# Last superblock of a hybrid decoder step: feed-forward tokens divided 512 + 320 instead of 384 + 448, final norm per piece

## The chip, the cores and the metric

The kernel runs on one core of one Trainium2 chip. The metric is device time in microseconds (us) of one execution, the median over several executions; lower is better. The profile names the engines PE (matrix multiply), PEld (its weight loads, which overlap the multiplies), DVE (vector), ACT (scalar), POOL (GpSimd) and SP (which issues the DMAs).

## The reference

One layer of a decoder trunk is computed for 2048 prompt tokens and 64 sample tokens, 1024 features each, all in fp32. The part that the change touches is the end of it:

```python
x = x + o @ w_co                      # end of the cross-attention
h = _rmsnorm(x, g_ffn)
x = x + jnp.square(jax.nn.relu(h @ w_up)) @ w_down     # hidden size 4096
...
y = _rmsnorm(x, g_final)
```

What comes before (a projection, windowed attention, a pooling mixer, cross-attention to 256 memory tokens) is not changed.

## The kernel before

Tokens stand along the free axis (columns), features on the 128 partitions, so x is 8 chunks of [128, tokens]. The tokens are worked through in three superblocks, each of two blocks (`SBLOCKS`): 384 + 384 tokens, then 256 + 256 with the 64 sample tokens, then 384 + 384. The residual x of a superblock lives in two SBUF tiles, `x_105` (block 0) and `x_106` (block 1). In the last superblock (s = 2) the 64 sample tokens, saved by superblock 1, are appended to block 1 in front of the feed-forward part, so that block 1 has `np` = 384 columns up to the cross stage and `nf` = 448 columns from there on.

Every fp32 product is made of three fp32r matmuls: weights and activations are each split into a rounded part (hi) and a remainder (lo), and hi*hi, hi*lo and lo*hi are summed in PSUM. In `dense` these are lines L317, L318, L319, in `mm3` lines L113, L114, L115. Each has its own 128x128 weight load. One weight tile pair (th, tl) of 128x1024 thus makes 24 matmuls for each block of tokens: 8 chunks of the contraction by 3 in `dense`; 2 output chunks of 4 contraction chunks by 3 in the down projection. I call these 24 matmuls a chunk.

The feed-forward part has groups g = 0 to 7. `up(g)` computes four hidden chunks for each feed-forward block `fb`; `down(g)` multiplies them by four weight tiles and adds them to x. The order is up(0), up(1), down(0), up(2), ..., up(7), down(6), down(7). In up(0), `head=2` does two chunks of one block, then two of the other; elsewhere the blocks alternate chunk by chunk. In down(7), the last, all four weight tiles are used for one block first, and then for the other, so that the first one's final norm runs beside the matmuls of the second. Before the change, superblock 2 has two feed-forward blocks that are the token blocks: 384 columns (block 0) and 448 (block 1); down(7) does block 1 first (`ends = (1, 0)`).

Each up chunk is evacuated by `up_evac`: DVE multiplies the relu of the PSUM tile by r3, the reciprocal norm of the tokens (L1192), ACT squares it (L1193) and rounds it (L1195), DVE makes the remainder (L1196). Down chunks are added to x by DVE (L1227). There are four PSUM tiles `mm` for the chunks. DVE and ACT also split each new weight tile (L135, L134).

`Act(n, nk)` lays out activations in SBUF tiles: pieces of 384 columns, four to a tile, for n up to 384, else pieces of 512 columns, three to a tile; `fb.more` lends the last feed-forward block of superblock 2 the tile `vt` and tiles of the weight pool `w` as additional room.

`Norm` sums squares of the 8 chunks. Off PE, ACT squares (L204, L207), DVE adds (L208), and one fp32 matmul by a matrix of ones (L216) sums over partitions. With `on_pe`, each square (L197) goes to PE at once (L200). `fin` then takes Ln and Exp on ACT (L219, L220) and a correction of three steps on DVE (L221 to L223). `final` applies it to the eight chunks of x on DVE (L1245) and issues four DMAs to y from SP (L1247).

Work that would stall an engine is put off: `later` holds pairs of a count and a function, and each `flush` counts down. `after_co(b)`, which finishes the norm r3 of block b, and `final` are put off in that way. The Tile framework then schedules the instructions on each engine by their dependencies; the order on an engine is fixed at build time.

Of the kernel before, what the change touches and what calls it, by code (L numbers as in the profile page):

```python
# [12 lines left out]
ALU = mybir.AluOpType  # L13
# [38 lines left out]
def kernel(ctx: ExitStack, tc: tile.TileContext, io, nW=12, nF=6, nT=8):  # L52
# [476 lines left out]
    def superblock(s, blks, nxt):  # L529
# [612 lines left out]
        def add_evac2(c, b, ps):  # L1142
            bl = blks[b]
            nc.vector.tensor_tensor(bl.x(c, 0, bl.np), ps[:, 0:bl.np], bl.x(c, 0, bl.np), ALU.add)
            fb, o = bl.fb, bl.fo
            gain(bl.xf(c), fb.h3.hi(c, o, o + bl.nf), fb.h3.lo(c, o, o + bl.nf), vec[:, V_GFFN + c:V_GFFN + c + 1])
            bl.norm.sq(c)

        def after_co(b):
# [3 lines left out]
            bl.norm.fin()  # L1153
            bl.r3 = bl.norm.r

        fbs = []
        for bl in blks:
            bl.norm = Norm(bl.nf, bl.xf)
            if not has or bl.b == 0:
                fb = FB()  # L1160
                fb.parts, fb.n, fb.more = [], 0, [(), (), ()]
                fbs.append(fb)
            bl.fb, bl.fo = fb, fb.n
            fb.parts.append(bl)
            fb.n += bl.nf
# [17 lines left out]
        def up_evac(g):  # L1183
            def f(c, b, ps):
                fb = fbs[b]
                if (g, b) not in hid:
                    hid[(g, b)] = Act(fb.n, 4, fb.more[1 + g % 2])
                H = hid[(g, b)]
                for bl in fb.parts:
                    o, n = bl.fo, bl.nf  # L1190
                    r, q = TS.get(), TS.get()
                    nc.vector.scalar_tensor_tensor(r[:, 0:n], ps[:, o:o + n], 0.0, bl.r3[:, 0:n], ALU.max, ALU.mult)  # L1192
# [12 lines left out]
        def down(g):  # L1205
            fin = g == 7
            nb = len(fbs)
            ends = (1, 0) if last else tuple(range(nb))
            seq = [(mp, b) for b in ends for mp in range(4)] if fin else [(mp, b) for mp in range(4) for b in range(nb)]
            loaded, left = {}, {}  # L1210
            if fin:
                for bl in blks:
                    bl.norm = Norm(bl.nf, bl.xf, on_pe=last and bl.b == 0)
            for mp, b in seq:
                if mp not in loaded:
                    loaded[mp] = S.next(("dn", s, g, mp))
# [5 lines left out]
                for m2 in range(2):  # L1222
                    m = 2 * mp + m2
                    ps = MM.get()
                    mm3(ps[:, 0:n], range(4), lambda k: w8(th)[:, 4 * m2 + k, :], lambda k: w8(tl)[:, 4 * m2 + k, :], H.hi, H.lo)
                    for bl in fb.parts:
                        nc.vector.tensor_tensor(bl.xf(m), ps[:, bl.fo:bl.fo + bl.nf], bl.xf(m), ALU.add)  # L1227
                        if fin:
                            bl.norm.sq(m)
# [11 lines left out]
        def final(bl):  # L1241
            bl.norm.fin()
            n, yo = bl.nf, 8 * bl.t0
            for k in range(8):
                nc.vector.scalar_tensor_tensor(bl.xf(k), bl.xf(k), vec[:, V_GFINAL + k:V_GFINAL + k + 1], bl.norm.r[:, 0:n], ALU.mult, ALU.mult)  # L1245
# [165 lines left out]
```

## Time and profile before

| what | value |
|---|---|
| median of 3 runs | 2584.61 us (2584.56 to 2587.79) |
| the profiled execution | 2587.05 us |
| its span, first to last instruction | 2585.3 us |
| PE busy | 2544.8 us, 98% of the span |
| DVE busy, ACT busy | 1376.7 us (53%), 994.1 us (38%) |
| mean granted PE clock | 0.994 of full speed |

The page's figures hold for the whole span; the feed-forward part of superblock 2 is the last 600 us or so of it (from 1981 us on). In the timeline a row gives start, duration, engine, line, operation, what it writes and reads, its shape. A matmul's duration is longer than the distance to the next one, since matmuls overlap in the array; the time that a matmul costs is the distance between starts.

### The profile page before, as it was taken

To read this page: it belongs to the slowest core of one execution; us is meant where nothing else is said; L and a number is where in the kernel's file an instruction comes from. 1 tells how busy PE (TensorE), PEld (TensorE's weight loads), DVE (VectorE), ACT (ScalarE), POOL (GpSimd) and SP (SyncE) were. 2 spreads that over 40 slices of the span, in tenths; PEclk is the share of its full clock that TensorE was granted. 3 is DMA by queue.
4 is the path that set the end of the run, shared out by engine and by line. 5 is a ranking of instruction groups with operands and counts; after the bars stand their busy time and mean duration, and the time that the engine had idled before them with its cause. 6 is when DMAs were issued, how large, how long until landed. Compare 5 with 4: busy or idle time off the path is not lost.

```text
span 2585.3 us, 35891 instructions
## 1 busy us (share of the span) xinstructions
PE 2544.8 (98%) x14239; PEld 2359.9 (91%) x14239; DVE 1376.7 (53%) x2643; ACT 994.1 (38%) x1931; POOL 169.4 (7%) x282
## 2 busy tenths in 40 slices
PE   8899999999999999999999999999999999999998
PEld 8798989999999999896888888899989999999997
DVE  8568535444434468763654546887445333333334
ACT  6666333322222234753442324475344322222221
POOL 0015010000000000411000000023010000000000
PEclk9999999999999999999999999999999999999999
DMA  7833212211112125156722222404111111111101
GB/s 283 257 125 105 87 36 82 66 66 63 61 66 66 50 65 159 50 175 212 274 97 98 98 98 74 157 24 145 41 66 62 61 58 58 57 58 58 58 25 53
DMA packets 96011, 245.06 MB, mean 95 GB/s; under 512 B 18852, under 2 KB 35684, under 8 KB 94820
## 3 DMA queue, kind: packets, MB, share of 16 engines
q1 hardware_dynamic: 95844, 242.78, 28.1%
q8 instruction: 112, 1.84, 0.3%
q14 instruction: 55, 0.45, 0.1%
HBM read 219.79 MB, written 22.95 MB: 94 GB/s over the span
## 4 chain that ended last, share of the span: by engine, by line
PE 56%; DVE 1%; ACT 1%; POOL 1%; DMA 1%; issue 0%; DVEq 0%; POOLq 0%; ACTq 0%
PE mm L318 10%; PE mm L319 10%; PE mm L317 10%; PE mm L113 7%; PE mm L114 7%; PE mm L115 7%; PE aux L724 1%; PE aux L755 1%; PE aux L1052 0%; DVE x L1245 0%; PE aux L968 0%; PE aux L113 0%; PE aux L115 0%; PE aux L114 0%; DVE w L135 0%
## 5 line engine op out<-in xcount | busy, mean ns | idle before, releaser
L317 PE MATMUL mm<-act,w 128*128 128x384 f32 (+4 forms) x2528 | 858.7, 340 | 2.0 <-ACT act L679 1.6
L319 PE MATMUL mm<-act,w 128*128 128x384 f32 (+4 forms) x2528 | 853.0, 337 | 1.9 <-DVE w L135 1.9
L318 PE MATMUL mm<-act,w 128*128 128x384 f32 (+4 forms) x2400 | 806.5, 336 | 0.2 <-DVE act L680 0.2
L134 ACT CAST w<-f 128x1024 fp32r<-128x1024 f32 x330 | 346.6, 1051 | 876.6 <-PE mm L114 281.2
L135 DVE TENSOR_TENSOR w<-f,w 128x1024 fp32r<-128x1024 f32 x330 | 402.8, 1225 | 221.2 <-PE mm L318 88.8
L113 PE MATMUL mm<-act,w 128*128 128x384 f32 (+3 forms) x1472 | 507.7, 345 | 3.9 <-ACT t L204 2.2
L115 PE MATMUL mm<-act,w 128*128 128x384 f32 (+3 forms) x1472 | 507.1, 345 | 1.9 <-DVE w L135 1.9
L317 PEld LDWEIGHTS mm<-act,w 128*128 128x128 f32 x2528 | 477.5, 189 | 21.4 <-ACT act L679 1.9
L319 PEld LDWEIGHTS mm<-act,w 128*128 128x128 f32 x2528 | 477.3, 189 | 17.3 <-DVE w L135 2.7
L318 PEld LDWEIGHTS mm<-act,w 128*128 128x128 f32 x2400 | 453.5, 189 | 17.5 <-issue 2.2
L114 PE MATMUL mm<-act,w 128*128 128x384 f32 (+3 forms) x1344 | 458.3, 341 | 0.0
L1227 DVE TENSOR_TENSOR x<-mm,x 128x384 f32<-128x384 f32 (+2 forms) x384 | 195.2, 522 | 294.9 <-PE mm L115 294.8
L113 PEld LDWEIGHTS mm<-act,w 128*128 128x128 f32 x1472 | 277.8, 189 | 20.7 <-ACT t L204 2.4
L115 PEld LDWEIGHTS mm<-act,w 128*128 128x128 f32 x1472 | 277.8, 189 | 17.9 <-DVE w L135 2.3
L114 PEld LDWEIGHTS mm<-act,w 128*128 128x128 f32 x1344 | 253.8, 189 | 12.9
L1192 DVE SCALAR_TENSOR_TENSOR t<-mm,t 128x384 f32<-128x384 f32 (+1 forms) x192 | 97.7, 522 | 225.2 <-PE mm L319 225.1
L1193 ACT ACTIVATE t<-t 128x384 f32<-128x384 f32 (+1 forms) x192 | 92.0, 493 | 204.8 <-DVE t L1192 204.8
L1196 DVE TENSOR_TENSOR act<-t,act 128x384 fp32r<-128x384 f32 (+2 forms) x176 | 87.7, 512 | 95.4 <-ACT act L1195 95.3
L113 PE MATMUL mm<-w,act 128*128 128x512 f32 x288 | 114.9, 403 | 2.4 <-ACT w L134 2.4
L114 PE MATMUL mm<-w,act 128*128 128x512 f32 x288 | 113.9, 396 | 1.4 <-DVE w L135 1.4
L115 PE MATMUL mm<-w,act 128*128 128x512 f32 x288 | 113.4, 394 | 0.0
L266 ACT ACTIVATE act<-x,vec 128x384 fp32r<-128x384 f32 (+3 forms) x96 | 56.4, 587 | 107.0 <-DVE x L940 56.8
(210 smaller groups left out, 2183.5 us busy)
## 6 DMA issues: line engine op xcount, KB each, us to landing
f<-in_wup SPq DMA_DIRECT2D x96, 512.0 KB, 3.3
f<-in_wdn SPq DMA_DIRECT2D x96, 512.0 KB, 3.3
f<-in_win SPq DMA_DIRECT2D x30, 512.0 KB, 3.5
f<-a_s SPq DMA_DIRECT2D x24, 512.0 KB, 4.3
f<-b_s SPq DMA_DIRECT2D x24, 512.0 KB, 4.3
x<-in_x SPq DMA_DIRECT2D x6, 1536.0 KB, 8.2
f<-in_wco SPq DMA_DIRECT2D x16, 512.0 KB, 5.4
f<-in_cmk SPq DMA_DIRECT2D x16, 512.0 KB, 4.4
```

Source lines behind the costliest of these rows:

```text
L113: nc.tensor.matmul(ps, Wh(k), Hh(k), start=first and i == 0, stop=False)
L114: nc.tensor.matmul(ps, Wh(k), Hl(k), start=False, stop=False)
L115: nc.tensor.matmul(ps, Wl(k), Hh(k), start=False, stop=final and i == last)
L134: nc.scalar.copy(th[:], r[:, 0:1024])
L135: eng.tensor_tensor(tl[:], r[:, 0:1024], f32(th[:]), ALU.subtract)
L317: nc.tensor.matmul(ps[:, 0:n], w8(th)[:, k, :], hi(b, k), start=k == 0, stop=False)
L318: nc.tensor.matmul(ps[:, 0:n], w8(th)[:, k, :], lo(b, k), start=False, stop=False)
L319: nc.tensor.matmul(ps[:, 0:n], w8(tl)[:, k, :], hi(b, k), start=False, stop=k == 7)
L1192: nc.vector.scalar_tensor_tensor(r[:, 0:n], ps[:, o:o + n], 0.0, bl.r3[:, 0:n], ALU.max, ALU.mult)
L1193: nc.scalar.activation(q[:, 0:n], r[:, 0:n], AF.Square)
L1196: nc.vector.tensor_tensor(lo, q[:, 0:n], f32(hi), ALU.subtract)
L1227: nc.vector.tensor_tensor(bl.xf(m), ps[:, bl.fo:bl.fo + bl.nf], bl.xf(m), ALU.add)
```

## The change

In superblock 2 the tokens are divided anew behind the cross stage: the first feed-forward block takes block 0 (384 columns) and the first 128 columns of block 1, together 512; the second takes the other 320 columns of block 1. A block of tokens now has parts `p`, each with a feed-forward block `p.fb`, an offset `p.o` in it, a column range from `p.c0` of `p.n` columns in x. The gain ahead of the feed-forward part, the up evacuation, the residual add, the final norm and the output DMAs go part by part. The extra room (`more`) goes to the first feed-forward block. In down(7) the 512 columns come first, and the 320 have their squares summed on PE. In up(0) of superblock 2, `early` now makes the deferred norm of block 1 run in front of the first evacuation. Superblocks 0 and 1 have one part per block, and the same instructions in the same order as before.

```diff
-            bl.xf = (lambda bl: lambda k: bl.xv[:, k, 0:bl.nf])(bl)
+            bl.xf = (lambda bl: lambda k, c0=0, c1=None: bl.xv[:, k, c0:bl.nf if c1 is None else c1])(bl)
...
-            fb, o = bl.fb, bl.fo
-            gain(bl.xf(c), fb.h3.hi(c, o, o + bl.nf), fb.h3.lo(c, o, o + bl.nf), vec[:, V_GFFN + c:V_GFFN + c + 1])
+            for p in bl.parts:
+                gain(p.x(c), p.fb.h3.hi(c, p.o, p.o + p.n), p.fb.h3.lo(c, p.o, p.o + p.n), vec[:, V_GFFN + c:V_GFFN + c + 1])
...
+            cut = {(1, 0): (256,), (1, 1): (256,), (2, 1): (128, 448)}.get((s, bl.b), (384,))
+            bl.parts, c0 = [], 0
+            for i, c1 in enumerate(cut):
...
+                p.fb = fbs[0] if has else fbs[i if last else bl.b]
+                p.o = p.fb.n
...
-            fb.more = [(vt, WS.get()), (WS.get(),), (WS.get(),)]
+            fbs[0].more = [(vt, WS.get()), (WS.get(),), (WS.get(),)]
...
-                for bl in fb.parts:
-                    o, n = bl.fo, bl.nf
+                for p in fb.parts:
+                    o, n = p.o, p.n
                     r, q = TS.get(), TS.get()
-                    nc.vector.scalar_tensor_tensor(r[:, 0:n], ps[:, o:o + n], 0.0, bl.r3[:, 0:n], ALU.max, ALU.mult)
+                    nc.vector.scalar_tensor_tensor(r[:, 0:n], ps[:, o:o + n], 0.0, p.bl.r3[:, p.c0:p.c0 + n], ALU.max, ALU.mult)
...
-                      head=2 if g == 0 else 0, tail=0, early=has and g == 0))
+                      head=2 if g == 0 else 0, tail=0, early=s > 0 and g == 0))
...
-            ends = (1, 0) if last else tuple(range(nb))
-            seq = [(mp, b) for b in ends for mp in range(4)] if fin else [(mp, b) for mp in range(4) for b in range(nb)]
+            seq = [(mp, b) for b in range(nb) for mp in range(4)] if fin else [(mp, b) for mp in range(4) for b in range(nb)]
...
-                for bl in blks:
-                    bl.norm = Norm(bl.nf, bl.xf, on_pe=last and bl.b == 0)
+                for fb in fbs:
+                    for p in fb.parts:
+                        p.norm = Norm(p.n, p.x, on_pe=last and fb is fbs[1])
...
-                    for i, bl in enumerate(fb.parts):
-                        later.append([DEFF[bl.b] + i, lambda bl=bl: final(bl)])
+                    for i, p in enumerate(fb.parts):
+                        later.append([DEFF[b] + i, lambda p=p: final(p)])
```

How the instructions stand on the engines, at the three places that matter. The lines below the diff are shifted by 8: L1192, L1196, L1227, L1245 of before are L1200, L1204, L1235, L1253 of the change. The last numbers in a row are the shape that is written.

DVE, one pair of up chunks in the middle of the feed-forward part, before (`mm` is PSUM, `t_103` and `t_98` are r3 of the two blocks):

```order
L1192 SCALAR_TENSOR_TENSOR t_97<-mm_107,t_103 128x384
L1196 TENSOR_TENSOR act_75<-t_101,act_77 128x384
L135 TENSOR_TENSOR w_86<-f_91,w_88 128x1024
L1192 SCALAR_TENSOR_TENSOR t_104<-mm_109,t_98 128x448
L1196 TENSOR_TENSOR act_68<-t_99,act_67 128x448
```

The same pair after the change:

```order
L1200 SCALAR_TENSOR_TENSOR t_98<-mm_107,t_103 128x384
L1200 SCALAR_TENSOR_TENSOR t_102<-mm_107,t_97 128x128
L1204 TENSOR_TENSOR act_75<-t_99,act_77 128x384
L1204 TENSOR_TENSOR act_75<-t_100,act_77 128x128
L135 TENSOR_TENSOR w_86<-f_91,w_88 128x1024
L1200 SCALAR_TENSOR_TENSOR t_104<-mm_109,t_97 128x320
L1204 TENSOR_TENSOR act_68<-t_101,act_67 128x320
```

The first block's evacuation is made of a 384 and a 128 part, the other's is 320 wide; the weight split between them stays.

DVE, from the last cross chunk (L1144 adds it to x) into up(0), before:

```order
L1144 TENSOR_TENSOR x_106<-mm_108,x_106 128x384
L135 TENSOR_TENSOR w_88<-f_93,w_82 128x1024
L267 SCALAR_TENSOR_TENSOR w_87<-x_106,vec,act_64 128x448
L208 TENSOR_TENSOR t_104<-t_104,t_100 128x448
L1192 SCALAR_TENSOR_TENSOR t_97<-mm_107,t_103 128x384
L1196 TENSOR_TENSOR act_76<-t_101,act_66 128x384
L221 SCALAR_TENSOR_TENSOR t_99<-t_98 128x448
L222 SCALAR_TENSOR_TENSOR t_99<-aux_111,t_99 128x448
L223 SCALAR_TENSOR_TENSOR t_98<-t_99,t_98 128x448
L1192 SCALAR_TENSOR_TENSOR t_102<-mm_109,t_103 128x384
```

After:

```order
L1144 TENSOR_TENSOR x_106<-mm_108,x_106 128x384
L267 SCALAR_TENSOR_TENSOR w_87<-x_106,vec,act_73 128x128
L267 SCALAR_TENSOR_TENSOR act_65<-x_106,vec,act_63 128x320
L208 TENSOR_TENSOR t_104<-t_104,t_100 128x448
L1200 SCALAR_TENSOR_TENSOR t_98<-mm_107,t_103 128x384
L1204 TENSOR_TENSOR act_76<-t_99,act_66 128x384
L221 SCALAR_TENSOR_TENSOR t_101<-t_97 128x448
L222 SCALAR_TENSOR_TENSOR t_101<-aux_111,t_101 128x448
L223 SCALAR_TENSOR_TENSOR t_97<-t_101,t_97 128x448
L1200 SCALAR_TENSOR_TENSOR t_102<-mm_107,t_97 128x128
L1204 TENSOR_TENSOR act_76<-t_100,act_66 128x128
L1200 SCALAR_TENSOR_TENSOR t_104<-mm_109,t_103 128x384
```

The gain's remainder (L267) is now two instructions, one for each feed-forward block, and the norm of block 1 (L221 to L223, 448 columns) stands ahead of the 128 part of the first evacuation, which needs it.

PE at the same place, before (the last matmuls of the first up chunk, the sum of block 1's squares, the second up chunk):

```order
L318 MATMUL mm_107<-act_74,w_79 128x384
L319 MATMUL mm_107<-act_72,w_80 128x384
L216 MATMUL aux_111<-t_104,ones 128x448
L317 MATMUL mm_109<-act_71,w_89 128x384
L318 MATMUL mm_109<-act_73,w_89 128x384
L319 MATMUL mm_109<-act_71,w_90 128x384
```

After:

```order
L318 MATMUL mm_107<-w_87,w_79 128x512
L319 MATMUL mm_107<-act_73,w_80 128x512
L216 MATMUL aux_111<-t_104,ones 128x448
L317 MATMUL mm_109<-act_71,w_89 128x512
L318 MATMUL mm_109<-act_73,w_89 128x512
L319 MATMUL mm_109<-act_71,w_90 128x512
```

The first two up chunks are 512 wide instead of 384, and the sum of squares stays behind the first of them.

DVE, the end of the program, before:

```order
L221 SCALAR_TENSOR_TENSOR t_103<-t_99 128x448
L222 SCALAR_TENSOR_TENSOR t_103<-aux_114,t_103 128x448
L223 SCALAR_TENSOR_TENSOR t_99<-t_103,t_99 128x448
L1245 SCALAR_TENSOR_TENSOR x_106<-x_106,vec,t_99 128x448 x8
L1227 TENSOR_TENSOR x_105<-mm_109,x_105 128x384
L1227 TENSOR_TENSOR x_105<-mm_110,x_105 128x384
L1227 TENSOR_TENSOR x_105<-mm_108,x_105 128x384
L221 SCALAR_TENSOR_TENSOR t_102<-t_104 128x384
L222 SCALAR_TENSOR_TENSOR t_102<-aux_112,t_102 128x384
L223 SCALAR_TENSOR_TENSOR t_104<-t_102,t_104 128x384
L1245 SCALAR_TENSOR_TENSOR x_105<-x_105,vec,t_104 128x384 x8
```

After, from the first finishing pass on (its L221 to L223 stand ahead of it as before, 384 wide):

```order
L1253 SCALAR_TENSOR_TENSOR x_105<-x_105,vec,t_102 128x384 x8
L1235 TENSOR_TENSOR x_106<-mm_109,x_106 128x320
L1235 TENSOR_TENSOR x_106<-mm_110,x_106 128x320
L1235 TENSOR_TENSOR x_106<-mm_108,x_106 128x320
L221 SCALAR_TENSOR_TENSOR t_97<-t_103 128x128
L222 SCALAR_TENSOR_TENSOR t_97<-aux_113,t_97 128x128
L223 SCALAR_TENSOR_TENSOR t_103<-t_97,t_103 128x128
L1253 SCALAR_TENSOR_TENSOR x_106<-x_106,vec,t_103 128x128 x8
L221 SCALAR_TENSOR_TENSOR t_104<-t_102 128x320
L222 SCALAR_TENSOR_TENSOR t_104<-aux_112,t_104 128x320
L223 SCALAR_TENSOR_TENSOR t_102<-t_104,t_102 128x320
L1253 SCALAR_TENSOR_TENSOR x_106<-x_106,vec,t_102 128x320 x8
```

Between the last three adds and the last finishing pass there is now a third pass, of 128 columns.

More of the change, by code (lines that the diff above doesn't have):

```diff
@@ L1154, in after_co @@
             bl.r3 = bl.norm.r
-        fbs = []
+        fbs = [FB() for _ in range(1 if has else 2)]
+        for fb in fbs:
+            fb.parts, fb.n, fb.more = [], 0, [(), (), ()]
         for bl in blks:
             bl.norm = Norm(bl.nf, bl.xf)
[L1159 to L1165, printed above, removed]
+            cut = {(1, 0): (256,), (1, 1): (256,), (2, 1): (128, 448)}.get((s, bl.b), (384,))
+            bl.parts, c0 = [], 0
+            for i, c1 in enumerate(cut):
+                p = FB()
+                p.bl, p.c0, p.n = bl, c0, c1 - c0
+                p.x = (lambda bl, c0, c1: lambda k: bl.xf(k, c0, c1))(bl, c0, c1)
+                p.fb = fbs[0] if has else fbs[i if last else bl.b]
+                p.o = p.fb.n
+                p.fb.n += p.n
+                p.fb.parts.append(p)
+                bl.parts.append(p)
+                c0 = c1
         if last:
             assert len(VS.free) == 4
-            fb.more = [(vt, WS.get()), (WS.get(),), (WS.get(),)]
+            fbs[0].more = [(vt, WS.get()), (WS.get(),), (WS.get(),)]
         for fb in fbs:
@@ L1207, in down @@
             nb = len(fbs)
-            ends = (1, 0) if last else tuple(range(nb))
-            seq = [(mp, b) for b in ends for mp in range(4)] if fin else [(mp, b) for mp in range(4) for b in range(nb)]
+            seq = [(mp, b) for b in range(nb) for mp in range(4)] if fin else [(mp, b) for mp in range(4) for b in range(nb)]
             loaded, left = {}, {}
             if fin:
-                for bl in blks:
-                    bl.norm = Norm(bl.nf, bl.xf, on_pe=last and bl.b == 0)
+                for fb in fbs:
+                    for p in fb.parts:
+                        p.norm = Norm(p.n, p.x, on_pe=last and fb is fbs[1])
             for mp, b in seq:
@@ L1225, in down @@
                     mm3(ps[:, 0:n], range(4), lambda k: w8(th)[:, 4 * m2 + k, :], lambda k: w8(tl)[:, 4 * m2 + k, :], H.hi, H.lo)
-                    for bl in fb.parts:
-                        nc.vector.tensor_tensor(bl.xf(m), ps[:, bl.fo:bl.fo + bl.nf], bl.xf(m), ALU.add)
+                    for p in fb.parts:
+                        nc.vector.tensor_tensor(p.x(m), ps[:, p.o:p.o + p.n], p.x(m), ALU.add)
                         if fin:
-                            bl.norm.sq(m)
+                            p.norm.sq(m)
                     MM.put(ps)
@@ L1235, in down, with final @@
                 if fin and mp == 3:
-                    for i, bl in enumerate(fb.parts):
-                        later.append([DEFF[bl.b] + i, lambda bl=bl: final(bl)])
+                    for i, p in enumerate(fb.parts):
+                        later.append([DEFF[b] + i, lambda p=p: final(p)])
             for b in range(nb):
                 hid.pop((g, b)).free()
-        def final(bl):
-            bl.norm.fin()
-            n, yo = bl.nf, 8 * bl.t0
+        def final(p):
+            p.norm.fin()
+            n, yo = p.n, 8 * (p.bl.t0 + p.c0)
             for k in range(8):
-                nc.vector.scalar_tensor_tensor(bl.xf(k), bl.xf(k), vec[:, V_GFINAL + k:V_GFINAL + k + 1], bl.norm.r[:, 0:n], ALU.mult, ALU.mult)
+                nc.vector.scalar_tensor_tensor(p.x(k), p.x(k), vec[:, V_GFINAL + k:V_GFINAL + k + 1], p.norm.r[:, 0:n], ALU.mult, ALU.mult)
                 if k % 2 == 1:
-                    nc.sync.dma_start(io["y"][:, yo + (k - 1) * n:yo + (k + 1) * n].rearrange("p (k n) -> p k n", n=n), bl.xv[:, k - 1:k + 1, 0:n])
+                    nc.sync.dma_start(io["y"][:, yo + (k - 1) * n:yo + (k + 1) * n].rearrange("p (k n) -> p k n", n=n), p.bl.xv[:, k - 1:k + 1, p.c0:p.c0 + n])
                     if has and k < 7:
                         yield
-            TS.put(bl.norm.r)
+            TS.put(p.norm.r)
         S.resF = 0
@@ L1394 @@
     ys = []
-    for sbk in SBLOCKS:
+    for sbk in SBLOCKS[:2] + [[(1280, 384, 0), (1664, 128, 0), (1792, 256, 64)]]:
         for t0, npr, _ in sbk:
```

## The prediction, made before the run

> **What bounds the kernel now.** I read the page first, then the stage that the change touches by windows, then single rows of the timeline for what a matmul of each width costs, and last the end of the program.
>
> ```profile
> span 2585.3 us, 35891 instructions
> PE 2544.8 (98%) x14239; PEld 2359.9 (91%) x14239; DVE 1376.7 (53%) x2643; ACT 994.1 (38%) x1931; POOL 169.4 (7%) x282
> 1990.39:2548.82 558.43, 558.43 (x2929) 530.65 (x2929) 217.11 (x311) 135.00 (x192) 0.00 (x0) 1.00 0.15 51
> ```
>
> The third line is a window (length; then busy time and count of PE, PEld, DVE, ACT, POOL; granted clock; DMA share; GB/s) from the first 448-wide up chunk of superblock 2 to the start of the last block of down(7). PE is busy for all 558.43 us at the full clock, DVE for 39% of them, ACT for 24%. So here the time is the sum of distances between matmul starts, and nothing else. What a chunk of 24 matmuls costs by width, from the starts of chunks:
>
> ```profile
> 1123.61 0.28 PE L317 MATMUL mm<-act,w 128*128 128x256 f32 x1
> 1126.49 0.31 PE L317 MATMUL mm<-act,w 128*128 128x320 f32 x1
> 1130.01 0.28 PE L317 MATMUL mm<-act,w 128*128 128x256 f32 x1
> ...
> 1345.00 0.39 PE L113 MATMUL mm<-act,w 128*128 128x512 f32 x1
> 1366.76 0.39 PE L317 MATMUL mm<-act,w 128*128 128x512 f32 x1
> ...
> 2009.32 0.34 PE L317 MATMUL mm<-act,w 128*128 128x384 f32 x1
> 2013.50 0.36 PE L317 MATMUL mm<-act,w 128*128 128x448 f32 x1
> 2018.43 0.34 PE L317 MATMUL mm<-act,w 128*128 128x384 f32 x1
> ...
> 2064.02 0.34 PE L113 MATMUL mm<-act,w 128*128 128x384 f32 x1
> 2073.14 0.34 PE L113 MATMUL mm<-act,w 128*128 128x384 f32 x1
> ```
>
> 256 columns: 2.88 us a chunk (120 ns each), 320: 3.52 (147), 384: 4.18 (174), 448: 4.93 (205), 512: 21.76 us for the four chunks of a down group in superblock 1, 5.44 each (227). 256 to 320 and 320 to 384 cost 27 ns a matmul, but 384 to 448 costs 31, and 448 to 512 only 21: a 448-wide matmul is 5 to 6 ns dearer than the line through the other four widths, and it is the only width that leaves it.
>
> **The change, part by part.**
>
> (a) Up chunks: 32 pairs. Before 2018.43 - 2009.32 = 9.11 us, after 5.44 + 3.52 = 8.96. That is -0.15 x 32 = -4.8 us.
>
> (b) Down chunks of groups 0 to 6: 28 pairs at 2073.14 - 2064.02 = 9.12, after 8.96: -0.16 x 28 = -4.5 us.
>
> Both price 512 and 320 by superblock 1, where the pieces lie as they will now (512-wide and 384-wide pieces). Superblock 1 doesn't show 512-wide matmuls that read from `vt` or `w`. The nearest rows are these, in the order 448 from `vt`, 448 from `w`, 512 from `act`, 512 from `w` in the prologue:
>
> ```profile
> L318 PE MATMUL mm<-vt,w 128*128 128x448 f32 x64 | 23.6, 369 | 0.0
> L114 PE MATMUL mm<-w,w 128*128 128x448 f32 x128 | 47.1, 368 | 0.0
> L113 PE MATMUL mm<-act,w 128*128 128x512 f32 x256 | 99.9, 390 | 0.0
> L113 PE MATMUL mm<-w,act 128*128 128x512 f32 x288 | 114.9, 403 | 2.4 <-ACT w L134 2.4
> ```
>
> In this stage the source makes no difference (368 to 369 ns, as from `act`), so I take 227 ns; the prologue's 13 ns longer is the upper end (a rival below).
>
> By the Trainium skill (TensorE: Matmul & The Clock Gate, Back-to-back issue gap), a warm stream's distance is N / 2.4 ns plus about 2.5 ns. By that rule 384 + 448 costs as much as 512 + 320, both 832 columns; (a) and (b) would be nothing, and the time about 2585, as before. The trace agrees on the slope (27 ns for 64 columns), not on the constant (120 ns at 256 leaves 13), and not at 448.
>
> (c) down(7), first block. It was 448 wide, now 512:
>
> ```profile
> 2524.03 0.36 PE L113 MATMUL mm<-act,w 128*128 128x448 f32 x1
> 2548.82 0.34 PE L113 MATMUL mm<-act,w 128*128 128x384 f32 x1
> ```
>
> These 24.79 us hold five chunks, 4.96 each. Four chunks now cost 5.44: +1.9 us.
>
> (d) The end, from the start of down(7)'s second block (2548.82), which becomes 320 wide instead of 384:
>
> ```profile
> 2561.72 0.92 PE L216 MATMUL aux<-t,ones 128*128 128x448 f32 x2
> 2564.02 0.62 DVE L221 SCALAR_TENSOR_TENSOR t<-t 128x448 f32<-128x448 f32 x1
> 2565.99 4.86 DVE L1245 SCALAR_TENSOR_TENSOR x<-x,vec,t 128x448 f32<-128x448 f32 x8
> 2570.01 0.34 PE L115 MATMUL mm<-act,w 128*128 128x384 f32 x1
> 2570.77 1.48 DVE L1227 TENSOR_TENSOR x<-mm,x 128x384 f32<-128x384 f32 x3
> 2571.93 2.20 PE L200 MATMUL aux<-t,ones 128*128 128x384 f32 x6 [1.59 <-ACT t L197]
> 2575.34 0.56 DVE L221 SCALAR_TENSOR_TENSOR t<-t 128x384 f32<-128x384 f32 x1 [3.09 <-ACT t L220]
> 2577.12 4.32 DVE L1245 SCALAR_TENSOR_TENSOR x<-x,vec,t 128x384 f32<-128x384 f32 x8
> ```
>
> DVE carries this end: PE's last product starts at 2570.01, but DVE is in the 448-wide finishing pass until 2570.85, and only then takes the last three adds. A pass (three corrections, eight products) takes 6.83 us for 448 columns (2564.02 to 2570.85) and 6.10 for 384 (2575.34 to 2581.44), so 0.73 for 64 columns; I extend that line to 5.37 for 320 and 3.18 for 128. Step by step:
> - To the first pass, 15.20 us. PE reaches L216 after 56 products and four sums L200: 56 x 27 ns = 1.5 us less, some 0.1 less for each narrower sum, 0.1 us back for each where PE would wait for the square (it waits little now, and the products in front of it shrink). L216, Ln and Exp are 384 wide instead of 448: 0.25 less. Together about -1.8.
> - First pass, 384 instead of 448: -0.7.
> - Three adds, 320 wide: -0.2.
> - From the adds to the last pass, now 3.09 us of waiting for squares, sums, Ln and Exp. In the new order the 128 pass stands in this place. Its own Ln and Exp come behind the last square on ACT (an estimate: three steps of 0.3 to 0.5 us), so DVE can start it some 1.2 us after the adds, and it takes 3.18: 4.4 us, +1.3. The sums, Ln and Exp of the 320 run beside it.
> - Last pass, 320: -0.7.
> - SP issues four DMAs more, beside DVE's passes (0.33 us each). The last DMA's landing stays at 2.0 to 2.9 us:
>
> ```profile
> DMA to landing us min/median/max: 2.0/2.4/4.1
> ```
>
> Together -2.1. Bounds: -3.6 if the 128 pass fits wholly into the old wait; +0.8 if it costs as much as a 384 pass (nearest row, +2.9).
>
> (e) The start of up(0). The first chunk now needs the gain of both blocks, and its evacuation the norm of both:
>
> ```profile
> 1981.60 0.55 DVE L1144 TENSOR_TENSOR x<-mm,x 128x384 f32<-128x384 f32 x1
> 1983.20 0.68 DVE L267 SCALAR_TENSOR_TENSOR w<-x,vec,act 128x448 fp32r<-128x448 f32 x1
> 1985.48 0.91 PE L216 MATMUL aux<-t,ones 128*128 128x448 f32 x2
> 1989.56 0.62 DVE L223 SCALAR_TENSOR_TENSOR t<-t,t 128x448 f32<-128x448 f32 x1
> ```
>
> The last cross chunk ends at about 1981.3 (its add starts at 1981.60). The gain's remainder is there at 1983.9. Split in two, DVE and ACT need perhaps 0.6 us more. PE wants it only for the last three of 24 matmuls, 21 x 0.227 = 4.8 us after 1981.3, at 1986.1: cover of 1.6 us. If that cover were gone, PE would wait 1 or 2 us once. The norm's result comes 4.7 us after its sum starts (1985.48 to 1990.18). After the change the sum starts 1.3 us later, behind a 5.44 us chunk, so the first evacuation waits until about 1992. Behind it in DVE's queue stand the next evacuations; who needs them is the fifth chunk, for its PSUM tile, at about 2000. I cost (e) at nothing.
>
> (f) The additional instructions. Per up pair DVE gets two of 128 columns, and per down pair two; ACT two per up pair. Widths add up as before, so each costs its fixed part alone:
>
> ```profile
> 2000.22:2037.00 36.78, 36.78 (x195) 35.10 (x194) 14.36 (x21) 13.10 (x21) 0.00 (x0) 1.00 0.18 57
> L1192 DVE SCALAR_TENSOR_TENSOR t<-mm,t 128x384 f32<-128x384 f32 x96 | 53.5, 558 | 145.0 <-PE mm L319 145.0
> L1192 DVE SCALAR_TENSOR_TENSOR t<-mm,t 128x256 f32<-128x256 f32 x64 | 24.4, 420 | 80.2 <-PE mm L319 80.2
> ```
>
> The line through 256 and 384 gives about 0.28 us at 128 and a fixed part of 0.14. In the window of four up pairs DVE is busy 14.36 of 36.78 us; it gains some 0.3 us a pair of 9. PE hides it, and would still with three times as much.
>
> Sum: -4.8 - 4.5 + 1.9 - 2.1 = -9.5 us. The profiled execution would go from 2587.05 to 2577.6. It lay 2.4 us over the median of 2584.61; from the median I get 2575.1 us, 0.37% less. About 0.2% (5.2 us) is what a measurement of this kernel tells from no change.
>
> **The rivals.**
>
> *The excess belongs to the stage, not to the width.* What speaks for it: all 448-wide matmuls of the program are in this stage. Then a pair stays at 9.1 us and (a) and (b) are nothing; +1.9 and, with the second block's products dearer as well (96 x 6 ns), some -1.5 are left: 2585.0. Against it: in the same stage 384 costs 174 ns, as elsewhere. By the rule of the Trainium skill (TensorE: Matmul & The Clock Gate, Back-to-back issue gap) the same time would come out.
>
> *Slower: 512-wide products are disturbed here as in the prologue.* This is where DVE and ACT write the `w` tiles that PE reads. At 13 ns more (403 against 390) for all 1536 of them it is +20 us: 2595. It decides from (9.5 + 5.2) us / 1536 = 9.6 ns on. Against it: at 448 the rows from `vt`, `w` and `act` don't differ, and superblock 1 ran a whole feed-forward part at 227 ns.
>
> *The gain is there, but the seams take it:* the 128 pass at its upper bound (+2.9), and 2 us of waiting in (e): 2580.0.
>
> **How the numbers follow.** The forecast has 0.84, and its own range is 2573.0 to 2578.2 (both bounds of (d), with half a microsecond for the measurement at the low end). Seams 0.05, excess of the stage 0.08, disturbed 512: 0.03. The range of 8 in 10 is 2572.8 to 2579.4, which leaves out the last two cases and part of the seams. Faster by over 0.2% (under 2579.4): 0.87. Within: 0.10. Slower: 0.03.
>
> **What would show it.** Chunks of 512 start 5.44 us apart from the next, 320 ones 3.52, and PE without idle from 1985 us on: (a), (b) right. 320 at 153 ns or 512 at 235 would make the prediction wrong by the first or second rival. PE idle before L318 in the first up chunk would show (e) wrong; a last finishing pass that starts more than 4.4 us after the last add, or a PE that ends after the first pass, would show (d) wrong.

## The result, and the profile after

| | median us | runs | ratio to before, 95% interval |
|---|---|---|---|
| before, same chip | 2584.56 | 7 (2583.38 to 2587.79) | |
| after | 2576.7 | 7 (2570.61 to 2580.2) | 0.9965 [0.9954, 0.9977] |
| after, timed once more with the last experiment | 2577.64 | 9 (2574.8 to 2581.33) | 0.9972 [0.9962, 0.9982] |

The change makes the kernel 7.9 us faster. The forecast was 2575.1 with a range of 2572.8 to 2579.4. The profiled execution of after took 2575.38 us. The head of its page, then two windows (columns as in the prediction's window): from the first 512-wide up chunk to 1985.50, inside the second one, and from there to the start of down(7)'s second block:

```profile
span 2573.6 us, 36150 instructions
PE 2534.6 (98%) x14241; PEld 2315.0 (90%) x14241; DVE 1388.7 (54%) x2797; ACT 998.9 (39%) x2013; POOL 167.4 (7%) x282
1977.45:1985.50 8.05, 8.05 (x35) 6.36 (x35) 4.08 (x8) 4.07 (x8) 0.00 (x0) 1.00 0.19 65
1985.50:2539.69 554.19, 554.19 (x2946) 493.33 (x2946) 228.30 (x448) 139.02 (x264) 0.00 (x0) 1.00 0.15 52
```

PE has no idle time in the stage here either, at the full clock. DVE runs 154 instructions more in the whole program and is busy 41% of the long window instead of 39%.

The two profiled executions may not be compared by their spans alone. The code ahead of the changed part is the same, but it ran faster in the profile of after, which lay 1.3 us under its median, while that of before lay 2.4 us over its own. The sum of block 0's squares, which stands in front of the last cross chunk, in the timeline of after and then of before:

```profile
1972.64 0.81 PE L216 MATMUL aux<-t,ones 128*128 128x384 f32 x2
```
```profile
1976.51 0.81 PE L216 MATMUL aux<-t,ones 128*128 128x384 f32 x2
```

These 3.87 us lie ahead of the change. I therefore measure from this sum on, to the start S of down(7)'s second block and from there to the last instruction:

| us | sum to S | S to the end | both |
|---|---|---|---|
| before | 572.31 | 36.46 | 608.77 |
| after | 567.04 | 33.93 | 600.97 |
| difference | -5.27 | -2.53 | -7.80 |

-7.80 agrees with the medians' -7.9. Measured so, the second profile of after gives 600.96: the part behind the sum repeats to 0.01 us.

Chunk starts of after, down and then up, in the timeline of PE:

```profile
2059.28 0.39 PE L113 MATMUL mm<-act,w 128*128 128x512 f32 x1
2064.75 0.30 PE L113 MATMUL mm<-act,w 128*128 128x320 f32 x1
2068.26 0.39 PE L113 MATMUL mm<-act,w 128*128 128x512 f32 x1
...
2086.22 0.39 PE L317 MATMUL mm<-act,w 128*128 128x512 f32 x1
2091.71 0.30 PE L317 MATMUL mm<-act,w 128*128 128x320 f32 x1
2095.23 0.39 PE L317 MATMUL mm<-act,w 128*128 128x512 f32 x1
```

A down pair takes 8.98 us and an up pair 9.01, against 9.12 and 9.11 before. 320 costs what was forecast (3.51 to 3.52), 512 does not: 5.47 in a down chunk and 5.49 in an up chunk instead of 5.44. The groups of the stage by shape show a first trace of why:

```profile
L113 PE MATMUL mm<-act,w 128*128 128x512 f32 x255 | 99.5, 390 | 0.0
...
L318 PE MATMUL mm<-vt,w 128*128 128x512 f32 x62 | 24.6, 397 | 0.0
L318 PE MATMUL mm<-w,w 128*128 128x512 f32 x62 | 24.1, 389 | 0.0
```

At 448 columns the row from `vt` (369 ns) lay 1 ns above the one from `act`; at 512 it is 7 to 8 ns above the rows shown here. The distances between starts in one up chunk of 512 (starting at 2086.22), in ns, show two places:

```
231 235 229 232 231 227 226 227 227 226 227 227 226 | 235 234 229 232 230 227 227 226 227 227
```

The first five, behind a 320, cost together some 25 ns more than five times 227; the five from the bar on, where `vt` is first read, 27 ns.

The end of after, in the timeline (the finishing pass's products are L1253 here, the residual add L1235):

```profile
2550.98 0.81 PE L216 MATMUL aux<-t,ones 128*128 128x384 f32 x2
2553.06 0.56 DVE L221 SCALAR_TENSOR_TENSOR t<-t 128x384 f32<-128x384 f32 x1 [0.16 <-ACT t L220]
2554.84 4.32 DVE L1253 SCALAR_TENSOR_TENSOR x<-x,vec,t 128x384 f32<-128x384 f32 x8
2559.07 1.28 DVE L1235 TENSOR_TENSOR x<-mm,x 128x320 f32<-128x320 f32 x3
2560.12 0.81 PE L200 MATMUL aux<-t,ones 128*128 128x320 f32 x2 [1.75 <-ACT t L197]
2561.92 0.29 DVE L221 SCALAR_TENSOR_TENSOR t<-t 128x128 f32<-128x128 f32 x1 [1.57 <-ACT t L220]
2562.82 0.47 ACT L220 ACTIVATE t<-t 128x320 f32<-128x320 f32 x1
2562.90 2.19 DVE L1253 SCALAR_TENSOR_TENSOR x<-x,vec,t 128x128 f32<-128x128 f32 x8
2565.00 0.48 DVE L221 SCALAR_TENSOR_TENSOR t<-t 128x320 f32<-128x320 f32 x1
2566.58 3.79 DVE L1253 SCALAR_TENSOR_TENSOR x<-x,vec,t 128x320 f32<-128x320 f32 x8
```

DVE carries this end too. It waits 1.57 us for the 128 columns' Exp, then runs both passes without a gap; the 320's Exp was done at 2563.29, 1.7 us before DVE came to it.

### The profile page after: what moved, and what is told of

The parts are those of the page before. It is cut to its first block, busy times and chain, and to the rows that moved or that the text cites. A ratio compares the mean times of both kernels' runs of the same rounds, so it can differ in the third digit from the quotient of the medians.

```text
span 2573.6 us, 36150 instructions
## 1 busy us (share of the span) xinstructions
PE 2534.6 (98%) x14241; PEld 2315.0 (90%) x14241; DVE 1388.7 (54%) x2797; ACT 998.9 (39%) x2013; POOL 167.4 (7%) x282
## 4 chain that ended last, share of the span: by engine, by line
PE 56%; DVE 2%; ACT 1%; DMA 1%; POOL 0%; issue 0%; DVEq 0%; POOLq 0%; ACTq 0%
PE mm L318 10%; PE mm L317 10%; PE mm L319 10%; PE mm L114 7%; PE mm L113 7%; PE mm L115 7%; PE aux L724 1%; PE aux L755 1%; DVE x L1253 0%; PE aux L968 0%; PE aux L1052 0%; PE aux L114 0%; DVE w L135 0%; PE aux L113 0%; PE aux L115 0%; PE aux L1090 0%
## 5 line engine op out<-in xcount | busy, mean ns | idle before, releaser
L317 PE MATMUL mm<-act,w 128*128 128x384 f32 (+3 forms) x2528 | 857.1, 339 | 2.5 <-ACT act L679 1.6
L319 PE MATMUL mm<-act,w 128*128 128x384 f32 (+3 forms) x2528 | 851.4, 337 | 1.9 <-DVE w L135 1.9
L318 PE MATMUL mm<-act,w 128*128 128x384 f32 (+3 forms) x2400 | 801.8, 334 | 0.7 <-DVE act L680 0.7
L113 PE MATMUL mm<-act,w 128*128 128x384 f32 (+3 forms) x1472 | 506.1, 344 | 3.2 <-ACT t L204 2.2
L115 PE MATMUL mm<-act,w 128*128 128x384 f32 (+3 forms) x1472 | 504.8, 343 | 1.9 <-DVE w L135 1.9
L114 PE MATMUL mm<-act,w 128*128 128x384 f32 (+3 forms) x1344 | 454.1, 338 | 0.0
L1235 DVE TENSOR_TENSOR x<-mm,x 128x384 f32<-128x384 f32 (+2 forms) x448 | 199.2, 468 | 297.3 <-PE mm L115 297.2
L1200 DVE SCALAR_TENSOR_TENSOR t<-mm,t 128x384 f32<-128x384 f32 (+3 forms) x224 | 99.8, 468 | 275.6 <-PE mm L319 275.5
L1201 ACT ACTIVATE t<-t 128x384 f32<-128x384 f32 (+3 forms) x224 | 95.1, 450 | 249.8 <-DVE t L1200 249.8
L1204 DVE TENSOR_TENSOR act<-t,act 128x384 fp32r<-128x384 f32 (+3 forms) x192 | 87.8, 477 | 88.9 <-ACT act L1203 88.9
```

The costliest lines, as they stand in the source:

```text
L113: nc.tensor.matmul(ps, Wh(k), Hh(k), start=first and i == 0, stop=False)
L114: nc.tensor.matmul(ps, Wh(k), Hl(k), start=False, stop=False)
L115: nc.tensor.matmul(ps, Wl(k), Hh(k), start=False, stop=final and i == last)
L317: nc.tensor.matmul(ps[:, 0:n], w8(th)[:, k, :], hi(b, k), start=k == 0, stop=False)
L318: nc.tensor.matmul(ps[:, 0:n], w8(th)[:, k, :], lo(b, k), start=False, stop=False)
L319: nc.tensor.matmul(ps[:, 0:n], w8(tl)[:, k, :], hi(b, k), start=False, stop=k == 7)
```

## The experiments

### Is it the width at all? (w448)

The change's whole structure, with parts per block, the new order at the end and the norms per part, but with the widths of before: 448 and 384.

```diff
- cut = {..., (2, 1): (128, 448)}
+ cut = {..., (2, 1): (64, 448)}
```

> The changed kernel with one number other: the first feed-forward block takes 64 columns of block 1 instead of 128, so that it is 384 + 64 = 448 wide and the second 384; three parts, three final norms and the order of the change stay. Theory W (the gain comes from the widths): a pair of chunks costs 9.11 to 9.12 us again, 60 pairs lose some 7.3 us against the change, the first block of down(7) is 1.96 us cheaper, the end about 2 us longer than with 320: 2584 us, the time of before within 1 us. Rival S (the gain comes from the new structure: norm of block 1 ahead of the evacuation, parts, 512 columns no part of it): about 2577, as the change.

Measured: 2584.22 us (12 runs), ratio 1.0001 [0.9992, 1.0011]. From the sum on it took 608.04 us, 0.7 less than before and all of it behind S. One pair of its up chunks (window: length, then busy time and count of PE and of the other engines as above):

```profile
2013.05:2022.16 9.11, 9.11 (x49) 8.69 (x48) 3.64 (x7) 3.31 (x7) 0.00 (x0) 1.00 0.17 59
```

9.11 us, as before. So the gain comes from the widths; the parts, the additional instructions and the moved passes cost nothing, and bring 0.7 us.

### What a width costs by itself (m1_widths)

A stream of chunks of 24 products with their weight loads, nothing beside it, from 256 to 512 columns. None of the kernel's own computation is in it.

> A kernel of its own: it computes nothing of the reference, it only streams chunks of 24 fp32r matmuls (each with its weight load, contraction 128) of one width after another, and writes what is left over to the outputs. It measures the distance between starts by width alone, without any other work of the layer. Theory W (the width itself costs it): distance = 13.3 ns + columns / 2.4 GHz, that is 120 at 256, 146.7 at 320, 173.3 at 384, 213.3 at 480, 226.7 at 512, but 206.7 and not 200 at 448, whatever the pitch of the pieces (448, 480 or 512 columns). Rival P (pitch): 448 wide pieces cost 206.7 only at pitch 512, and 200 at pitch 448 or 480. Rival S (the stage): 448 lies on the line here, 200 ns, because no DVE, ACT or DMA traffic runs beside it. For the first matmuls of 512 after a narrower width, the changed kernel shows 229 to 235 ns for five matmuls, some 25 ns a chunk in all; if that comes from the change of width it stands here too, in the alternating chunks; and if the tile from which the remainders are read costs anything, it stands in the last chunks.

Mean distance between starts, ns, and what it lies over the line 13.3 + N / 2.4:

| columns | 256 | 320 | 384 | 400 | 416 | 432 | 440 | 448 | 456 | 480 | 496 | 512 |
|---|---|---|---|---|---|---|---|---|---|---|---|---|
| ns | 120.0 | 146.7 | 173.3 | 180.0 | 188.3 | 195.8 | 200.0 | 202.6 | 208.9 | 216.7 | 223.3 | 226.7 |
| over the line | 0 | 0 | 0 | 0 | 1.7 | 2.5 | 3.3 | 2.6 | 5.6 | 3.3 | 3.3 | 0 |

Every width tried from 416 to 504 lies above the line, so 448 is no special case, and theory W was wrong at 480 too. Of the widths that the table leaves out, 352 lies on the line, 424, 464 and 504 lie 3.3 ns above it, and 288 lies 1.7 ns under it (131.7). And 448 has more than one price. Three chunks of it at the same width and pitch, first behind 440, then later in the stream:

```profile
180.75:195.34 14.59, 14.59 (x73) 13.53 (x73) 1.86 (x3) 0.00 (x0) 0.00 (x0) 1.00 0.01 1
319.08:333.94 14.86, 14.86 (x73) 13.51 (x72) 1.88 (x3) 0.00 (x0) 0.00 (x0) 1.00 0.00 1
```

72 products lie in each: 202.6 ns a product, then 206.4 (206.7 once it is steady, as in the kernel before). The pitch of the pieces (the distance between their starts in a tile) can't be what parts these two, it is 512 columns in both; at a pitch of 448 it took 202.7, at 480 between 203.2 and 204.1. Between 416 and 504 most widths were tried behind their narrower neighbour alone, so others than 448 may have a second price too. The alternating chunks showed the rest: 512 behind 320 starts with 231, 236, 228, 233, 230 ns, in a stream where nothing else runs. The last chunks, whose remainders lie in two other tiles, near and far, took 5.44 us like the rest.

### Another width between (s480)

480 and 352, the rest as in the change.

```diff
- cut = {..., (2, 1): (128, 448)}
+ cut = {..., (2, 1): (96, 448)}
```

> The changed kernel with 96 columns of block 1 in the first feed-forward block: 480 + 352. Theory W in its narrow form (448 alone is dear): a pair costs 24 x (213.3 + 160.0) ns = 8.96 us and what the change of width costs, so within 1 us of the change: 2576 to 2578. Rival (every width between 384 and 512 carries 6.7 ns more, say because it isn't a multiple of 128 columns and over 384): a pair 9.12 us, 2584 to 2585.

Measured: 2579.93 us (11 runs), ratio 0.9984 [0.9975, 0.9992]; between both expectations. Its chunk starts:

```profile
2086.02 0.38 PE L317 MATMUL mm<-act,w 128*128 128x480 f32 x1
2091.22 0.33 PE L317 MATMUL mm<-act,w 128*128 128x352 f32 x1
2095.08 0.38 PE L317 MATMUL mm<-act,w 128*128 128x480 f32 x1
```

480 takes 5.20 us a chunk, 216.7 ns, what the bare stream gave and 3.3 ns over the line. Its pair is 9.06 us, halfway between before and after. That is the table above again, inside the kernel.

### Does DVE carry the end? (t1)

The first block's two finishing passes come one weight tile earlier, so that DVE does more of them while PE still has products to do.

```diff
- DEF, DEFF = (1, 1), (2, 2)
+ DEF, DEFF = (1, 1), (1, 2)
```

> The changed kernel with the first two finishing passes put off by one weight tile less (they are due after the first and second weight tile of down(7)'s second block instead of the second and third). Theory D (DVE carries the end: its passes of 384 and 128 stand in front of the last adds and of the last pass): the 384 pass starts about 5 us earlier, three of its four late adds are no longer held up, the 128 pass starts before the last add, and the end comes 1 to 3 us earlier than with the change: 2574 to 2576. Rival: the adds of the second block are held up by the earlier pass, PE waits for the squares that its sums need, and the products end later by what DVE gains: 2577 or more.

Measured: 2575.39 us (5 runs), ratio 0.9965 [0.9953, 0.9977]. The times alone don't part it from after; the trace does. From the sum to S 567.04 us, the same; from S to the end 31.79 instead of 33.93. Its end in the timeline:

```profile
2550.19 4.32 DVE L1253 SCALAR_TENSOR_TENSOR x<-x,vec,t 128x384 f32<-128x384 f32 x8
2558.26 2.19 DVE L1253 SCALAR_TENSOR_TENSOR x<-x,vec,t 128x128 f32<-128x128 f32 x8
2559.42 0.31 PE L115 MATMUL mm<-act,w 128*128 128x320 f32 x1
2560.36 0.48 DVE L1235 TENSOR_TENSOR x<-mm,x 128x320 f32<-128x320 f32 x1
2563.31 0.49 DVE L221 SCALAR_TENSOR_TENSOR t<-t 128x320 f32<-128x320 f32 x1 [2.46 <-ACT t L220]
2564.88 3.79 DVE L1253 SCALAR_TENSOR_TENSOR x<-x,vec,t 128x320 f32<-128x320 f32 x8
```

PE's last product now starts 19.31 us behind S, 0.94 later than in after, and the end still comes 2.14 earlier. So DVE's passes set the end, and PE's finish does not. The wait that the change had filled (2.46 us, for the last square, sum, Ln and Exp) is open again, and is now the end's next limit. Outside its span each of its executions has 2.1 us instead of 1.8, so 1.8 us of the 2.14 reach the time.

### Why 512 missed 5.44 (snake, vtalign, vtswap)

Each of these three was executed once, in 2575.58, 2570.56 and 2572.39 us. Single executions of after differ by more than the parts that are sought here, so I compare from the sum to S in the traces.

`snake` takes the two blocks in alternating order from up(1) to down(6), so that 512 follows 512 every second time:

```diff
+ seq=[(c, b ^ c % 2) for c in range(4) for b in (0, 1)] if last and g else None
- [(mp, b) for mp in range(4) for b in range(nb)]
+ [(mp, b ^ (mp % 2 if last else 0)) for mp in range(4) for b in range(nb)]
```

> In the last superblock's feed-forward, from up(1) to down(6), every second chunk takes its two blocks in the other order (512, 320, 320, 512, 512, 320, ...), so the width goes from 320 to 512 half as often: 28 of the 56 entries into 512 are gone. Theory E (the first five matmuls of 512 behind a change of width cost some 25 ns more a chunk in all): the 28 chunks of 512 that stand behind another 512 take 24 x 226.7 = 5.44 us where they read no vt (down) and some 5.47 where they do (up), those behind a 320 stay at 5.465 and 5.49, and the stretch from up(1) to down(6) is 28 x 0.025 = 0.7 us shorter. Rival (a chunk of 512 starts slowly whatever stood ahead of it, as a cost of its own first matmuls): every chunk of 512 keeps 5.465 or 5.49 and the stretch its length to 0.2 us. A third: two chunks of one width in a row make VectorE late, and TensorE waits for a PSUM buffer; then idle time of TensorE ahead of some chunks, 0.1 us and more each.

Sum to S: 566.48 us, 0.56 less than after. Starts where the order changes, in its timeline (between the second and the third row lie two chunks of 320, between the third and the fourth two of 512):

```profile
2086.91 0.39 PE L317 MATMUL mm<-act,w 128*128 128x512 f32 x1
2092.38 0.30 PE L317 MATMUL mm<-act,w 128*128 128x320 f32 x1
2099.41 0.39 PE L317 MATMUL mm<-act,w 128*128 128x512 f32 x1
2110.37 0.30 PE L317 MATMUL mm<-act,w 128*128 128x320 f32 x1
```

The first of these chunks stands behind 512-wide down products and takes 5.47 us; the pair behind 320 takes 10.96, 5.49 and 5.47. Down chunks of 512 behind 512 take 5.44. A 320 behind a 320 takes 3.520 instead of 3.515, which gives back 28 x 0.005 of the 28 x 0.025 us: 0.56 expected, 0.56 measured. PE never waited.

`vtalign` allocates `vt` ahead of the small tiles of odd column counts; `vtswap` lets `vt` and a weight tile change places as holders of the last four remainders:

```diff
# vtalign
+ vt = sb("vt", 1024, F32R)
  ident = sb("ident", P)
...
- vt = sb("vt", 1024, F32R)
# vtswap
- fbs[0].more = [(vt, WS.get()), ...]
+ fbs[0].more = [(WS.get(), vt), ...]
```

> The tile vt is allocated ahead of the small tiles of odd sizes, so that it stands elsewhere in SBUF; nothing else changes. Theory A (the five slow matmuls from the first read of vt in each up chunk, 27 ns, come from the place of vt): up chunks of 512 fall from 5.492 to 5.465 us, over 32 chunks 0.9 us. Rival (they come from something else at the fifth step of an up chunk, as what the other engines do then): 5.49 stays.

> vt and the weight tile that hold the last four remainders of the 512 block change places: remainders 4 and 5 now come from the weight tile, 6 and 7 from vt. If vt is what disturbs, the five slow matmuls of an up chunk move from the fifth k-step (matmul 14 of 24) to the seventh (matmul 20); if it is the step, they stay where they are; if neither, as where the read moves from a tile of activations to any other region for the first time, they stay at the fifth as well and vt's own read shows nothing. The length of a chunk stays 5.49 us in each case.

The matmuls that read `vt` in the stage (count; least, median, greatest ns), of vtalign and of vtswap, and two chunk starts of vtalign:

```profile
L318 PE MATMUL mm<-vt,w x60: 389/389/389, 1995.2 to 2471.8; 128*128 128x512 f32 x60
...
2082.05 0.39 PE L317 MATMUL mm<-act,w 128*128 128x512 f32 x1
2087.52 0.31 PE L317 MATMUL mm<-act,w 128*128 128x320 f32 x1
```
```profile
L318 PE MATMUL mm<-vt,w x62: 397/397/397, 1985.1 to 2475.0; 128*128 128x512 f32 x62
```

In another place `vt` is read like any other tile, the up chunk takes 5.465 us, and the sum to S is 566.19, 0.85 less than after. In its old place it is slow at whatever step it is read: in vtswap the slow matmuls moved to the 20th of the chunk (234, 235, 229, 232 ns), and the weight tile read at the 14th showed 227. Its sum to S is 567.04, as in after.

### The stream alone, in the kernel's order (m2_place)

The bare stream again, with 448 and 384 in turn, 512 and 320 in turn, and with remainders read from a tile at small shifts.

> A stream of chunks of 24 products as in m1_widths, with nothing beside it; none of the kernel's own computation. First chunks of 512 whose last four remainders (matmuls 14, 17, 20 and 23 of a chunk) are read from a tile at 0, 1, 2, 4, 5, 8, 16 and 32 columns from its start. Theory A (what disturbed the up chunks is the place of vt, behind tiles of odd sizes): at 0 and at large shifts a chunk takes 5.44 us, at some small shifts 24 x 226.7 ns and some 27 ns more, from matmul 14 on, and the table says from which shift on the place is harmless. Rival: it needs a narrower width or another engine's traffic, and all take 5.44. Then 448 alternating with 384 as in the kernel before: theory H (a 448 matmul takes 202.6 or 206.7 ns by what ran ahead of it) expects 206 to 208 ns there, 4.95 us a chunk, as in the kernel; if 448 behind 384 takes 202.6, the kernel's 206.7 is from what runs beside it. 448 behind 384 steadily, behind 440 and behind 512 tell which of them sets it: 4.86 us a chunk in one state, 4.96 in the other.

One pair of 448 and 384, one of 512 and 320; the second to the fourth chunk of 448 in a row behind 384, the same behind 512; three of 512 unshifted, three with the last four remainders 16 columns off:

```profile
201.35:210.47 9.12, 9.12 (x50) 8.67 (x49) 1.18 (x2) 0.00 (x0) 0.00 (x0) 1.00 0.01 2
371.21:380.19 8.98, 8.98 (x50) 8.02 (x49) 1.18 (x2) 0.00 (x0) 0.00 (x0) 1.00 0.00 0
251.11:266.00 14.89, 14.89 (x74) 13.51 (x72) 1.88 (x3) 0.00 (x0) 0.00 (x0) 1.00 0.00 1
311.21:325.80 14.59, 14.59 (x73) 13.52 (x72) 1.87 (x3) 0.00 (x0) 0.00 (x0) 1.00 0.00 0
49.34:65.66 16.32, 16.32 (x73) 13.52 (x72) 2.08 (x3) 0.00 (x0) 0.00 (x0) 1.00 0.00 1
148.42:164.98 16.56, 16.56 (x73) 13.52 (x72) 2.07 (x3) 0.00 (x0) 0.00 (x0) 1.00 0.00 1
```

9.12 and 8.98 are the kernel's own down pairs before and after, to the hundredth. Nothing that runs beside PE in the kernel is needed to explain them. 448 took 206.7 ns behind 384, and 202.6 behind 512, for four chunks on end. Shifts of the remainders by 1 to 32 columns all cost something: 5.47 to 5.55 us a chunk, where no shift costs nothing (5.44). So none of these shifts is harmless; theory A had expected that of the large ones. None shows just the five slow matmuls of `vt` either. That its place costs the 27 ns is shown by vtalign; what it is about the place is open.

The first pair of 448 and 384, where 448 still stood behind 512, and the next:

```profile
192.31:201.36 9.05, 9.05 (x49) 8.69 (x48) 1.32 (x2) 0.00 (x0) 0.00 (x0) 1.00 0.00 0
201.36:210.48 9.12, 9.12 (x49) 8.67 (x49) 1.18 (x2) 0.00 (x0) 0.00 (x0) 1.00 0.01 2
```

So at the lower price of 448 the pair would take 9.05 us, and half of the 0.14 us between 9.12 and 8.98 hangs on what stood ahead of it.

### All three together (best, after_b, best_b)

> All three together: finishing passes of the first block one weight tile earlier, every second chunk in the other order, vt elsewhere. By the sums of theories D, E and A: 2.1 us (measured in the trace of the run with the earlier passes), 0.7 and 0.9 under the changed kernel's 2576.7, so 2573.0 us, ratio 0.9955. If only the earlier passes count: 2574.6. If two 512 chunks in a row make VectorE late: 2577 and more.

> The changed kernel itself once more, beside the next one, so that both are timed on one chip in turn. 2576.7 us as before, ratio 0.9965.

> The three edits together once more, timed in turn with the changed kernel. If what the trace of the first run adds up to (2.14 us from the earlier passes, 0.56 from the order of the blocks, 0.85 from the place of vt) is what a run gains, its median lies 3.5 us under that of the changed kernel timed here. If the lower median of the first run was the work ahead of the changed part, which differs by some microseconds between runs, the two medians lie within 1 us.

| | median us | runs | ratio | sum to S | S to the end |
|---|---|---|---|---|---|
| best | 2570.91 | 6 (2568.38 to 2579.5) | 0.9959 [0.9946, 0.9973] | 565.63 | 31.79 |
| after_b | 2577.64 | 9 (2574.8 to 2581.33) | 0.9972 [0.9962, 0.9982] | 567.04 | 33.92 |
| best_b | 2577.22 | 6 (2573.89 to 2579.32) | 0.9970 [0.9959, 0.9982] | 565.63 | 31.78 |

In both profiles the part behind the sum is 3.55 us shorter than in after, which is 2.14 + 0.56 + 0.85, so the three add up. The times don't show it: timed in turn, both kernels have the same median within 0.5 us, the second of the two outcomes that were named for best_b. In best_b the code ahead of the sum, which is the same in all of them but for the place of `vt`, took 1977.9 us instead of 1971.3 in best and 1972.1 in after_b; from 900 to 1200 us its granted clock was 0.97, against 0.99 and 0.98. The runs best and best_b are of one kernel, so the place of `vt` alone can't make the difference between these two. But the mean granted clock of best_b's six executions was 0.992 to 0.995, half of them at 0.992, and that of after_b's nine 0.994 to 0.997, so whether the lower clock is chance or belongs to this version is open. Of the 3.55 us, 0.3 go to the time outside the span, as in t1. I don't call this version faster than the change.

## Why the prediction was right, and where it was off

| step | forecast us | measured us | how |
|---|---|---|---|
| (a) 32 up pairs | -4.8 | -3.4 | 9.11 to 9.007 |
| (b) 28 down pairs | -4.5 | -3.9 | 9.12 to 8.980 |
| (c) first block of down(7) | +1.9 | +1.96 | four chunks 19.83 to 21.79 |
| (d) the end | -2.1 | -2.53 | S to the end |
| (e), (f) | 0 | +0.1 | what is left |
| sum | -9.5 | -7.8 | |

**(a) and (b), the size.** The mechanism held: w448 takes the gain away by changing the widths back, and the bare stream shows both pair times. The term that was mis-sized is the 5.44 us a chunk, taken from superblock 1's down(7), where four chunks of 512 follow each other and `vt` isn't read. Behind a 320 a chunk of 512 costs 0.025 us more, and in an up chunk `vt` another 0.027, while a 320 behind a 512 is 0.005 cheaper than 3.52. That is 32 x 0.047 + 28 x 0.020 = 2.1 us, which is what (a) and (b) missed. snake and vtalign each took such a part away and got its price back. The prediction had read that the source makes no difference at 448. One row of before that it didn't show differs, by 5 ns:

```profile
L318 PE MATMUL mm<-w,w 128*128 128x448 f32 x64 | 23.3, 364 | 0.0
```

These are the products that follow the read of `vt` in an up chunk, where 448 has its lower price.

**The reason given for it was too simple.** The prediction said that 448 is the only width that leaves the line. m1_widths found every width from 416 to 504 above it, and 448 itself at 202.6 or 206.7 ns. Half of the gain of a down pair hangs on 448 standing behind 384, where it takes the higher price (9.12 and not 9.05 us in m2_place); the other half is there at the lower price too. The first rival (the excess is the stage's, not the width's) thus fell in its result, since 512 + 320 in the same stage is cheaper, but it had a true part: the excess does not belong to the width alone.

**By the rule** of the Trainium skill (TensorE: Matmul & The Clock Gate, Back-to-back issue gap), N / 2.4 + 2.5 ns, no gain would have come. The section calls it the gap of a single isolated matmul and says that at large N it counts too much for a stream with weight loads; the prediction took it for the distance in a warm stream. The runs agree with its slope at 256, 320, 384, 400 and 512 columns, and put the constant at 13.3 ns for these products, each with its own weight load, so here the rule counts too little: an estimated 215.8 ns at 512 columns by it, where m1_widths measured 226.7. The straight line does not hold from 416 to 504, nor at 288, and its bend at 448 is where the gain is.

**(c)** is the 512 chunk at 5.44 where it follows itself: right, for the reason given.

**(d)** Its steps, measured: S to the first pass 13.4 us (forecast 15.2 - 1.8); the adds to the 128 pass 1.57 us (1.2); that pass 3.08 (3.18); the last pass 5.37 (5.37). All within 0.4. The claim that the 320's sums, Ln and Exp run beside the 128 pass held, with 1.7 us to spare; so the 128 pass does hold up the end, and t1, which moved it away, gained. From the last add to the last pass it is 2565.00 - 2560.35 = 4.65 us, a little over the 4.4 that the prediction named as the limit, by the longer wait for ACT. S to the end of the last pass fell from 32.62 to 30.68 us, by 1.94. The other 0.6 of the -2.53 is a step that the prediction had at nothing: from the end of the last pass to the last instruction, in which the last DMA is issued and lands, it is 3.84 us before and 3.24 after (3.23 in t1, 3.28 in s480 with 352 columns, 3.44 in w448 with 384). Why it is shorter is open; before and w448 have the same width there, so the width isn't all of it. That the sum came as near as -7.8 is thus in part luck: this step made up for 0.6 of the 2.1 us that (a) and (b) missed.

Two bounds of the prediction don't follow from its steps. Without the 1.3 us of the 128 pass they give -3.4 and not -3.6, and 2575.1 + 2.9 is 2578.0 and not 2578.2. Nothing hung on either.

**(e)** Nothing waited: PE is busy for all 8.05 us of the short window above. The second part's first evacuation came at 1987.75, which is 1991.6 in the time of before; forecast was about 1992.

**(f)** held in w448, which has the additional instructions and no loss. The slower rival (512 disturbed by 13 ns each as in the prologue) did not appear: reads of `w` show 389 ns, those of `act` 390. What was seen at `vt`, 5 ns over five matmuls, is far under the 9.6 ns for every matmul from which it would have decided.

## What to carry to other kernels

Where a window of the profile shows PE without a gap, price a matmul by the distance of starts and measure it for each width, in the order in which the widths will follow each other: here the same 832 columns cost 9.12 us a pair as 448 + 384, 9.06 as 480 + 352 and 8.98 as 512 + 320. A price taken from chunks of one width on end leaves out what the change of width costs. And where one engine's passes follow the last product, ask whether they can start earlier before asking how to make the products faster.

## What the runs showed of the hardware that was not expected

- 448-wide products with the same operands take 202.6 ns each behind 512 and 206.7 behind 384, and stay so for at least four chunks (m2_place). In the kernel before, up chunks went from the one to the other midway: 207 ns up to the read of `vt`, some 203 at the end. That the read is what moved them wasn't tested. Behind 440 both were seen, 202.6 in one stream and 206.7 in the other. What sets the price is open.
- A change of width costs the first matmuls behind it: 512 behind 320 25 ns over five, 512 behind 384 41 ns over the first nine, 384 behind 448 28 ns or 6, depending on which of the two prices the 448 had; 320 behind 512 none.
- The place of an operand in SBUF counts. Reading the last four remainders of a chunk from a tile shifted by 1, 2, 4, 5, 8, 16 or 32 columns made some of the chunk's last eleven matmuls up to 14 ns longer, and after shifts of 2, 4 and 16 also the start of the next chunk; `vt`, allocated behind tiles of odd column counts, cost 27 ns a chunk until it was moved.
- The part of the program that is bound by PE repeats to 0.01 us between executions, while the part ahead of it differed by 6.6 us between two profiles of one kernel. A gain of 3.5 us in the first was not to be seen in the medians.
